# Keeping the low parts of twice-used weights, and five smaller rearrangements, in a two-block kernel on one core

## The chip, the cores and the metric

The kernel runs on one NeuronCore of one Trainium2 chip. A core has five engines with a queue of instructions each: TensorE (PE in the profile; its weight loads are listed as PEld), VectorE (DVE), ScalarE (ACT), GpSimd (POOL) and SyncE (SP). Here SP issues every large transfer between the chip's memory and the core's on-chip memory; sixteen DMA engines carry them out. The metric is the device time of one execution in microseconds, lower is better.

## The reference, cut to what matters

The input is x of 1024 tokens by 1024 features in fp32. Two blocks follow each other.

Block one: an RMS norm, one projection `w_in`, gated linear attention with 4 heads (64 key, 128 value features; decay per key feature, in the reference by chunks), a short causal convolution, the output projection `w_out`; then a gated FFN of 2816 hidden features (`w_gate_upffn`, `w_down`); then a gate `sigmoid(u3 @ w_ple_gate) * (p @ w_ple_proj)`; each added to the residual.

Block two: a layer norm, one projection `w_in_2` whose columns feed three mixers (spatial gating; a 31-tap convolution with its own layer norm over 256 channels; windowed attention with a bias by relative position), `w_out_2`, a residual and a last layer norm.

```
log_a = log_sigmoid(g_lr @ w_gate_up + b_gate) / 16
o     = causal attention of q, k, v with decay exp(cumsum(log_a))
y     = layer_norm(conv31(a * sigmoid(b)) + conv_b); yb = silu(y) * silu(gate)
```

## The kernel before, in words

Activations lie with features on the 128 partitions and 512 tokens (a half, `hf` 0 or 1) in the free dimension. fp32 products are made of three products in a faster format: each operand is split into a high part (rounded) and a low part (the rest), and `mm3` (lines 294 to 296) multiplies high by high, high by low, low by high. A product of a 1024 by 128 weight with a half is 24 matmuls of 128x512, which one reads off the profile as 24 starts in some 5.45 us; here that is called a gemm.

Weights come through the class `Weights`, in the order of a plan that is written out beforehand. `load` sends one weight (512 KB) from memory to one of three raw buffers on SP's queue; `split` makes the high part on ScalarE (line 104) and the low part on VectorE (line 105) into one of three pairs of buffers `hi` and `lo`; `ahead` splits one weight ahead of its gemm. Because a half is worked through before the other begins, `w_in`, `w_out`, `w_ple_gate` and 16 pieces of `w_in_2` stand in the plan twice and are loaded and split twice.

The order of work: `norm_in` and `proj` for half 0; then `proj` of half 1 interleaved with the attention `gla` of both halves; `out_proj` of half 0 beside what is left of `gla`; `out_proj` of half 1, beside `first_operands`; `ple_proj` beside `other_operands` (operands of the FFN: sums and differences of the two halves, each split); `ffn_up` and `ffn_down`; `ple` of half 0, then `ple` of half 1 beside `norm_mid` of half 0 (the norm that ends block one and begins block two); `mix2`, which interleaves the gemms of `w_in_2` with `norm_mid` of half 1, `spill_x2` (transposes of the residual, written to memory) and `conv31`, and ends with `conv_out`; then attention units with the last gemms (`late_tiles`) and `finish`. `run_both(a, b, na, nb)` interleaves two generators in the ratio na to nb.

What is written is an order of preference: the tile framework plans each engine's queue from it with a timing model of its own (`schedule_with_timeline_sim=True`), so an instruction may stand in its queue earlier or later than in the text. On the chip every queue runs in the order planned.

In `gla`, a chunk of 128 tokens takes two groups `g` of two heads. `exps` makes the decay factors E and multiplies: line 650 writes `qpad`, q times E for seven levels and each head of the pair apart (14 instructions of 64x64 per group; the other head's partitions hold zeros set once by line 618). `scores` first copies q into `qdiag`, a tile with zeros off the head's own partitions (line 666, GpSimd, 4 copies per chunk).

`ple_proj` begins with `load_pT`: it loads p (1 MB, line 1054), transposes it on TensorE (line 1064) and splits it. `setup2` makes a row of bias values and copies it to 128 rows for each of 8 heads, memory to memory (line 1168). `conv_out` (from line 1320) norms half 0 and then half 1: a sum over channels by a matmul with ones, the subtraction of the mean, squares (their addition on GpSimd, line 776), a second sum, `rsqrt` (lines 337 to 355), and the product with the gate.

Of the kernel before, what the change touches and what calls it, by code (L numbers as in the profile page):

```python
# [20 lines left out]
NH = 512  # L21
# [43 lines left out]
class Weights:  # L65


    RAW, SPLIT = 3, 3

    def __init__(self, nc, ctx, tc, plan):  # L70
        self.nc, self.plan = nc, plan
        self.pool = ctx.enter_context(tc.tile_pool(name="wts", bufs=1))
        self.raw, self.done = {}, {}
        self.n_raw = self.n_split = self.n_used = 0

    def load(self):
        i = self.n_raw
# [12 lines left out]
        self.raw[i] = t  # L90
        self.n_raw += 1

    def split(self):
        i = self.n_split
        if i >= len(self.plan):
            return
        while self.n_raw <= i:
            self.load()
        name, src, r0, kc, c0, m = self.plan[i]
        n = kc * m  # L100
        t = self.raw.pop(i)
        hi = self.pool.tile([128, WIDTH], F32R, tag=f"hi{i % self.SPLIT}", name=f"wh{i}")
        lo = self.pool.tile([128, WIDTH], F32R, tag=f"lo{i % self.SPLIT}", name=f"wl{i}")
        self.nc.scalar.activation(out=hi[:, :n], in_=t[:, :n], func=ACTF.Copy)  # L104
        self.nc.vector.tensor_tensor(out=lo[:, :n], in0=t[:, :n], in1=hi[:, :n].bitcast(F32), op=ALU.subtract)  # L105
        self.done[i] = (hi[:, :n].rearrange("p (k m) -> p k m", k=kc), lo[:, :n].rearrange("p (k m) -> p k m", k=kc))
        self.n_split += 1
        self.load()

    def get(self, *spec):  # L110
# [25 lines left out]
class Kernel:  # L136
    def __init__(self, tc, ctx, I, out, dbg):
        self.tc, self.nc, self.ctx, self.I, self.out, self.dbg_out = tc, tc.nc, ctx, I, out, dbg or {}
        nc = self.nc
        self.cst = ctx.enter_context(tc.tile_pool(name="cst", bufs=1))  # L140
        self.wts = Weights(nc, ctx, tc, self.weight_plan())
# [8 lines left out]
        self.dram = ctx.enter_context(tc.tile_pool(name="scr", bufs=1, space=DRAM))  # L150
# [445 lines left out]
    def gla_setup(self):  # L596
        nc, I = self.nc, self.I
        mask = self.temp([128, 448], "mask")
        nc.sync.dma_start(out=mask, in_=I["c_mask"])
        self.mask = mask.rearrange("p (l t) -> p l t", l=7).bitcast(U32)  # L600
        self.expm = self.temp([128, 1152], "expm", dtype=F32R)
        e = self.temp([128, 9, 128], "E", 2)
        nc.sync.dma_start(out=e, in_=I["c_expm"].rearrange("p (a b) -> p a b", a=9))
        nc.vector.tensor_copy(out=self.expm, in_=e.rearrange("p a b -> p (a b)"))
        self.wgu = self.temp([17, 256], "wgu")
        nc.sync.dma_start(out=self.wgu[0:16, :], in_=I["w_gate_up"][0])
        nc.sync.dma_start(out=self.wgu[16:17, :], in_=I["b_gate"])
        self.glr = self.temp([17, NH], "glr")
        nc.gpsimd.memset(self.glr, 1.0)
        self.state = self.temp([128, 2, 256], "state")  # L610
        nc.gpsimd.memset(self.state, 0.0)
        self.neg_gn = self.cst.tile([128, 1], F32, name="neg_gn")
        nc.vector.tensor_scalar(out=self.neg_gn, in0=self.v("gn_g"), scalar1=-1.0, scalar2=None, op0=ALU.mult)
        self.carry = self.temp([128, 8], "carry")
        self.qpad = [self.temp([128, 7, 2, 64], f"qpad{i}") for i in range(2)]
        self.qdiag = [self.temp([128, 2, 2, 128], f"qdiag{i}") for i in range(2)]
        for t in self.qpad + self.qdiag:
            nc.gpsimd.memset(t, 0.0)

    def gla(self, hf, R):  # L620
# [11 lines left out]
            return ap.rearrange("p g (b u n) -> p g b u n", u=2, n=n)[:, :, :, 1, :]  # L632

        def exps(c):
            for g in range(2):
# [9 lines left out]
                tok = slice(c * 128, (c + 1) * 128)  # L645
                q = qk[:, g, tok]
                for l, n in enumerate(GLA_LEVELS):
                    for par in range(2):
                        r = slice(64 * par, 64 * par + 64)
                        nc.vector.tensor_tensor(out=qs[r, l, par, :].rearrange("p (b n) -> p b n", n=n),  # L650
                                                in0=right(E[r, 1 + l, :], n), in1=right(q[r], n), op=ALU.mult)
                ql = self.temp([128, 128], "Q", 2)
                nc.vector.tensor_tensor(out=ql, in0=E[:, 8, :], in1=q, op=ALU.mult)
                k = qk[:, 2 + g, tok].rearrange("p (a t) -> p a t", a=1).to_broadcast([128, 8, 128])
                nc.vector.tensor_tensor(out=E[:, 0:8, :], in0=E[:, 0:8, :], in1=k, op=ALU.mult)
                qt = (qs, ql)
                KQ[c, g] = (E, qt)
                yield

        def scores(c):  # L660
            sT = self.temp([128, 4, 128], "sT", 2)
            tok = slice(c * 128, (c + 1) * 128)
            qd = self.qdiag[c % 2]
            for h in range(4):
                r = slice(64 * (h % 2), 64 * (h % 2) + 64)
                nc.gpsimd.tensor_copy(out=qd[r, h // 2, h % 2, :], in_=qk[r, h // 2, tok])
# [206 lines left out]
        yield from step("S4", s4)  # L873
        self.release(a11, a12)

    def ple_proj(self):

        nc, W = self.nc, self.wts
        pt = self.load_pT()
        yield  # L880
        for m in range(8):
            if m % 4 == 0:
# [47 lines left out]
    def ffn_up(self, A):  # L930
# [15 lines left out]
        for f in range(NF):  # L946
# [25 lines left out]
            nc.vector.tensor_tensor(out=u2, in0=u2, in1=s1, op=ALU.mult)  # L972
            nc.sync.dma_start(out=self.sT[f, :, 0, :], in_=u2)
            B = nxt
        for t in A.values():
            self.release(*t)
        self.release(self.up_last, *self.up_slots)
# [156 lines left out]
    def spill_x2(self, hf, N):  # L1134
# [3 lines left out]
        for t in range(4):  # L1138
            for k in range(2):
                ps = self.psx()  # L1140
                for j in range(4):
                    nc.tensor.transpose(ps[:, j * 128:(j + 1) * 128], h[k][:, j, t * 128:(t + 1) * 128], self.ident)
# [8 lines left out]
    def setup2(self):  # L1151
# [15 lines left out]
        for h in range(8):  # L1167
            nc.sync.dma_start(out=scr[h], in_=self.bias_row[h:h + 1, :].to_broadcast([128, 512]))
# [150 lines left out]
    def conv_out(self, ypad):  # L1319
# [1 line left out]
        nc = self.nc  # L1321
        a = self.cacc
        self.yb = self.bg
        for hf in range(2):
            sl = slice(hf * NH, (hf + 1) * NH)
            s = self.t512()
            nc.vector.tensor_tensor(out=s, in0=a[:, 0, sl], in1=a[:, 1, sl], op=ALU.add)
            ps = self.psx()
            self.colsum(ps, s, True)
            for ct in range(2):  # L1330
                nc.vector.scalar_tensor_tensor(out=a[:, ct, sl], in0=ps, scalar=-1.0 / 256, in1=a[:, ct, sl],
                                               op0=ALU.mult, op1=ALU.add)
            acc = self.t512()
            for ct in range(2):
                self.square_acc(acc, a[:, ct, sl], ct == 0)
            ps = self.psx()
            self.colsum(ps, acc, True)
            r = self.t512()
            self.rsqrt(r, ps, 1.0 / 256, 1e-5)
            for ct in range(2):  # L1340
# [195 lines left out]
    def run(self):  # L1536
# [3 lines left out]
        with self.banks_by(g=4, x=4):  # L1540
# [16 lines left out]
            with self.scope(4):  # L1557
# [3 lines left out]
                steps = self.out_proj(1, R[1], N[1])  # L1561
                next(steps)
                self.spill_h(0, N[0])
                run_both(steps, self.first_operands(N[0], A), 8, 8)
                self.spill_h(1, N[1])
                run_both(self.ple_proj(), self.other_operands(N, A), 18, 15)
                self.release(self.stat)
                self.ffn_up(A)
                self.ffn_down(N)
            with self.scope(5):  # L1570
                self.statz = self.slot([128, 2, NH], F32, "statz", base=True)
                for _ in self.ple(0, N[0]):
# [78 lines left out]
```

## Time and profile before

| | |
|---|---|
| median of 3 runs | 1714.7 us (1714.58 to 1716.91) |
| the profiled execution | 1713.7 us, of which the span from first to last instruction is 1711.7 us |
| busy share of the span | PE 97%, PEld 81%, DVE 67%, ACT 45%, POOL 20% |
| mean granted TensorE clock | 0.987 of full speed |
| moved by DMA | 199.83 MB, mean 117 GB/s |

TensorE is nearly always busy, so the time is its work plus the gaps in it. Its clock has two levels, 2.4 and 1.2 GHz; a granted clock of 0.66 over a stretch means that for two thirds of the stretch it was at half speed. A gap costs its own length, and what is run at 1.2 GHz after it.

### The profile page before, as it was taken

The numbers are of one execution on the slowest core, as the hardware profiler recorded it, in microseconds if no ns is written. First come the engines' busy times: TensorE is split into PE (matmuls) and PEld (weight loads), VectorE is DVE, ScalarE is ACT, GpSimd is POOL, SyncE is SP. The second block draws the span as 40 slices with busy tenths as digits, with TensorE's granted clock in tenths as the row PEclk, the third lists the DMA queues.
The fourth block names the chain that finished last, engine by engine and source line by source line (L and its number), as shares of the span: only waits on it lengthen the run. The fifth ranks groups of instructions, "written<-read, shape, count | busy, mean of one in ns | idle before, by whom it ended". The sixth has DMA issues, their size and how long they took to land.

```text
span 1711.7 us, 21055 instructions
## 1 busy us (share of the span) xinstructions
PE 1660.5 (97%) x7865; PEld 1379.6 (81%) x7865; DVE 1139.7 (67%) x1774; ACT 768.0 (45%) x1219; POOL 347.4 (20%) x293
## 2 busy tenths in 40 slices
PE   8999999999989999999999999999979999989998
PEld 6888987788767888888888888888858898878876
DVE  4255876996897645565554444237997799566997
ACT  5533346334555333333333433224677532476663
POOL 2010100200037534443330002003000010022443
PEclk9999999999999999999999999999989999999999
DMA  9333222223633222222226961342432521434111
GB/s 283 85 99 123 76 63 62 87 87 115 220 136 100 93 91 81 80 81 92 81 92 253 371 210 64 111 136 80 142 120 80 185 62 38 123 111 185 50 64 60
DMA packets 209501, 199.83 MB, mean 117 GB/s; under 512 B 9270, under 2 KB 173512, under 8 KB 207864
## 3 DMA queue, kind: packets, MB, share of 16 engines
q1 hardware_dynamic: 209400, 198.49, 35.7%
q8 instruction: 62, 1.02, 0.2%
q14 instruction: 39, 0.32, 0.1%
HBM read 157.56 MB, written 43.01 MB: 117 GB/s over the span
## 4 chain that ended last, share of the span: by engine, by line
PE 88%; DVE 7%; ACT 2%; issue 1%; DMA 1%; POOL 0%; SPq 0%; DVEq 0%; ACTq 0%; POOLq 0%
PE g L295 20%; PE g L294 20%; PE g L296 20%; PE x L294 6%; PE x L296 6%; PE x L295 6%; PE x L678 1%; PE s L1426 1%; PE t L1457 1%; PE o L1464 1%; PE x L640 1%; DVE wl L105 1%; DVE qpad L650 1%; PE x L366 1%; PE x L700 0%
## 5 line engine op out<-in xcount | busy, mean ns | idle before, releaser
L294 PE MATMUL g<-ah,wh 128*128 128x512 f32 x896 | 354.2, 399 | 11.3 <-issue 8.8
L295 PE MATMUL g<-al,wh 128*128 128x512 f32 x896 | 353.9, 396 | 0.4 <-DVE al L318 0.4
L296 PE MATMUL g<-ah,wl 128*128 128x512 f32 x896 | 353.5, 396 | 0.0
L104 ACT ACTIVATE wh<-wr 128x1024 fp32r<-128x1024 f32 (+1 forms) x142 | 150.3, 1062 | 284.8 <-PE g L295 167.5
L105 DVE TENSOR_TENSOR wl<-wr,wh 128x1024 fp32r<-128x1024 f32 (+1 forms) x142 | 181.2, 1278 | 137.5 <-ACT wh L104 133.6
L294 PEld LDWEIGHTS g<-ah,wh 128*128 128x128 f32 x896 | 169.5, 190 | 49.8 <-issue 11.2
L295 PEld LDWEIGHTS g<-al,wh 128*128 128x128 f32 x896 | 169.6, 189 | 37.5 <-issue 1.9
L296 PEld LDWEIGHTS g<-ah,wl 128*128 128x128 f32 x896 | 169.4, 189 | 37.3 <-issue 2.2
L315 DVE TENSOR_TENSOR s<-sr,s 128x1024 fp32r<-128x1024 f32 x36 | 43.8, 1223 | 69.1 <-ACT s L314 69.1
L914 POOL TENSOR_TENSOR sr<-wr,wr 128x512 f32<-128x512 f32 x22 | 47.0, 2138 | 178.3 <-DMA wr<-w_gate_upffn 142.6
L1316 DVE SCALAR_TENSOR_TENSOR cacc<-ypad,vec,cacc 128x1024 f32<-128x1024 f32 x60 | 76.1, 1293 | 0.4
L959 POOL TENSOR_TENSOR t<-t,t 128x512 f32<-128x512 f32 x22 | 39.9, 1815 | 173.4 <-ACT t L942 173.4
L314 ACT ACTIVATE s<-sr 128x1024 fp32r<-128x1024 f32 x36 | 37.8, 1054 | 77.8 <-PE x L296 59.3
L776 POOL TENSOR_TENSOR stat<-t,stat 128x512 f32<-128x512 f32 x14 | 23.5, 1703 | 234.6 <-ACT t L775 234.6
L295 PE MATMUL g<-s,wh 128*128 128x512 f32 x176 | 68.5, 389 | 0.0
L296 PE MATMUL g<-s,wl 128*128 128x512 f32 x176 | 68.5, 389 | 0.0
L295 PE MATMUL x<-s,wh 128*128 128x512 f32 x176 | 68.5, 389 | 0.0
L296 PE MATMUL x<-s,wl 128*128 128x512 f32 x176 | 68.5, 389 | 0.0
L294 PE MATMUL g<-s,wh 128*128 128x512 f32 x176 | 67.5, 389 | 0.0
L294 PE MATMUL x<-s,wh 128*128 128x512 f32 x176 | 67.5, 389 | 0.0
L650 DVE TENSOR_TENSOR qpad<-E,qk 64x64 f32<-64x64 f32 x224 | 51.4, 229 | 9.1 <-ACT E L642 6.3
L296 PE MATMUL g<-wh,al 128*128 128x256 f32 (+1 forms) x192 | 55.0, 288 | 0.0
(366 smaller groups left out, 3916.4 us busy)
## 6 DMA issues: line engine op xcount, KB each, us to landing
wr<-w_in SPq DMA_DIRECT2D x86, 512.0 KB
wr<-w_gate_upffn SPq DMA_DIRECT2D x44, 512.0 KB
sr<-sT SPq DMA_DIRECT2D x36, 512.0 KB
sT<-t SPq DMA_DIRECT2D x44, 256.0 KB
wr<-w_down SPq DMA_DIRECT2D x22, 512.0 KB
wr<-w_out SPq DMA_DIRECT2D x16, 512.0 KB
w2s<-w SPq DMA_DIRECT2D x8, 1024.0 KB
wr<-w_ple_gate SPq DMA_DIRECT2D x16, 512.0 KB
```

The source lines that it names most:

```text
L104: self.nc.scalar.activation(out=hi[:, :n], in_=t[:, :n], func=ACTF.Copy)
L105: self.nc.vector.tensor_tensor(out=lo[:, :n], in0=t[:, :n], in1=hi[:, :n].bitcast(F32), op=ALU.subtract)
L294: mm(out=ps, lhsT=lh, rhs=rh, start=start and i == 0, stop=False)
L295: mm(out=ps, lhsT=lh, rhs=rl, start=False, stop=False)
L296: mm(out=ps, lhsT=ll, rhs=rh, start=False, stop=stop and i == n - 1)
L314: nc.scalar.activation(out=hi, in_=src, func=ACTF.Copy)
L315: (eng or nc.vector).tensor_tensor(out=lo, in0=src, in1=hi.bitcast(F32), op=ALU.subtract)
L650: nc.vector.tensor_tensor(out=qs[r, l, par, :].rearrange("p (b n) -> p b n", n=n), in0=right(E[r, 1 + l, :], n), in1=right(q[r], n), op=AL ...
L776: (eng or nc.gpsimd).tensor_tensor(out=acc, in0=sq, in1=acc, op=ALU.add)
L914: nc.gpsimd.tensor_tensor(out=t13[:, 0, :], in0=b12, in1=b11, op=ALU.subtract)
L959: nc.gpsimd.tensor_tensor(out=v5, in0=v5, in1=z7, op=ALU.add)
L1316: nc.vector.scalar_tensor_tensor(out=acc, in0=src, scalar=w, in1=acc, op0=ALU.mult, op1=ALU.add)
```

## The change

Weights: when a weight stands in the plan a second time, the low part of its first use is stored in memory after the split (`keep`) and loaded into the `lo` buffer for the second use (`load_low`, asked for one weight ahead); VectorE makes no low part then. By the plan this is so for 24 pieces of `w_in`, 8 of `w_out`, 8 of `w_ple_gate` and 16 of `w_in_2`. In `gla` the copies into `qdiag` move from `scores` to the head of `exps`, and one multiplication of 128x(2x64) per level takes both heads from `qdiag`, zeros included, in place of two of 64x64. `load_pT` is called before `out_proj` of half 1 goes on. The bias copies move into `ffn_up`, one for each of f = 2 to 9. The first of each four transposes of `spill_x2` is kept in program order. `conv_out` takes each step for both halves before the next step, and its additions of squares go to VectorE. The interleaving of `ple(1)` with `norm_mid(0)` goes from 8:18 to 7:18.

```diff
@@ class Weights
+        for i, (name, _, *spec) in enumerate(plan):
+            key = (name, *spec)
+            if key in seen:
+                t = dram.tile([128, spec[1] * spec[3]], F32, name=f"low{i}")
+                self.kept[seen[key]] = self.again[i] = t
+            seen[key] = i
+    def load_low(self, i):
+        if i in self.again and i not in self.low:
+            _, _, _, kc, _, m = self.plan[i]
+            t = self.low[i] = self.low_tile(i)
+            self.nc.sync.dma_start(out=t[:, :kc * m].bitcast(F32), in_=self.again[i])
+    def keep(self):
+        if self.to_keep is not None:
+            i, lo = self.to_keep
+            self.nc.sync.dma_start(out=self.kept[i], in_=lo.bitcast(F32))
+            self.to_keep = None
@@ def split
             self.load()
+        self.keep()
...
         self.nc.scalar.activation(out=hi[:, :n], in_=t[:, :n], func=ACTF.Copy)
-        self.nc.vector.tensor_tensor(out=lo[:, :n], in0=t[:, :n], in1=hi[:, :n].bitcast(F32), op=ALU.subtract)
+        self.load_low(i)
+        lo = self.low.pop(i, None)
+        if lo is None:
+            lo = self.low_tile(i)
+            self.nc.vector.tensor_tensor(out=lo[:, :n], in0=t[:, :n], in1=hi[:, :n].bitcast(F32), op=ALU.subtract)
+            if i in self.kept:
+                self.to_keep = i, lo[:, :n]
...
         self.n_split += 1
+        self.load_low(i + 1)
         self.load()
@@ def gla_setup
-        for t in self.qpad + self.qdiag:
+        for t in self.qdiag:
             nc.gpsimd.memset(t, 0.0)
@@ def gla: exps (the same loop of copies leaves scores)
+            qd = self.qdiag[c % 2]
+            for h in range(4):
+                r = slice(64 * (h % 2), 64 * (h % 2) + 64)
+                nc.gpsimd.tensor_copy(out=qd[r, h // 2, h % 2, :], in_=qk[r, h // 2, tok])
...
-                    for par in range(2):
-                        r = slice(64 * par, 64 * par + 64)
-                        nc.vector.tensor_tensor(out=qs[r, l, par, :].rearrange("p (b n) -> p b n", n=n),
-                                                in0=right(E[r, 1 + l, :], n), in1=right(q[r], n), op=ALU.mult)
+                    e = E[:, 1 + l:2 + l, :].to_broadcast([128, 2, 128])
+                    nc.vector.tensor_tensor(out=qs[:, l].rearrange("p g (b n) -> p g b n", n=n),
+                                            in0=right(e, n), in1=right(qd[:, g], n), op=ALU.mult)
@@ def ffn_up (and the loop over 8 heads leaves setup2)
+            if 2 <= f < 10:
+                nc.sync.dma_start(out=self.bias_scr[f - 2], in_=self.bias_row[f - 2:f - 1, :].to_broadcast([128, 512]))
@@ def spill_x2
+                    if j == 0:
+                        self.tc.keep_in_program_order(ins)
@@ def conv_out
-        for hf in range(2):
+        for sl in halves:
             s = self.t512()
...
-                self.square_acc(acc, a[:, ct, sl], ct == 0)
+                self.square_acc(acc, a[:, ct, sl], ct == 0, nc.vector)
...
+        for sl, ps in zip(halves, accs):
             r = self.t512()
             self.rsqrt(r, ps, 1.0 / 256, 1e-5)
@@ def run
                 self.spill_h(0, N[0])
+                pt = self.load_pT()
                 run_both(steps, self.first_operands(N[0], A), 8, 8)
                 self.spill_h(1, N[1])
-                run_both(self.ple_proj(), self.other_operands(N, A), 18, 15)
+                run_both(self.ple_proj(pt), self.other_operands(N, A), 18, 15)
...
-                run_both(self.ple(1, N[1]), self.norm_mid(0, N[0]), 8, 18)
+                run_both(self.ple(1, N[1]), self.norm_mid(0, N[0]), 7, 18)
```

## Rows read from the trace of the kernel before

**Rows 1.** The page: span, busy time by engine, engines on the chain of waits.

```profile
span 1711.7 us, 21055 instructions
...
PE 1660.5 (97%) x7865; PEld 1379.6 (81%) x7865; DVE 1139.7 (67%) x1774; ACT 768.0 (45%) x1219; POOL 347.4 (20%) x293
...
PE 88%; DVE 7%; ACT 2%; issue 1%; DMA 1%; POOL 0%; SPq 0%; DVEq 0%; ACTq 0%; POOLq 0%
```

**Rows 2.** Busy time by stretch: length, busy by engine (instructions), granted clock, DMA share, GB/s.

```profile
5.00:35.00 30.00, 27.61 (x119) 22.13 (x120) 15.72 (x26) 21.85 (x35) 2.04 (x2) 1.00 1.04 333
285.00:320.00 35.00, 30.80 (x125) 23.04 (x124) 33.56 (x67) 19.48 (x26) 7.83 (x8) 0.95 0.27 80
350.00:365.00 15.00, 13.36 (x72) 11.61 (x71) 14.54 (x28) 7.10 (x15) 1.29 (x1) 0.89 0.42 141
440.00:455.00 15.00, 12.86 (x43) 8.14 (x42) 10.69 (x16) 5.15 (x7) 0.00 (x0) 0.89 0.75 254
475.00:520.00 45.00, 35.53 (x137) 25.75 (x136) 41.05 (x61) 24.89 (x43) 20.41 (x5) 0.92 0.37 131
...
1265.00:1285.00 20.00, 9.34 (x26) 5.36 (x26) 18.56 (x30) 16.51 (x25) 0.00 (x0) 0.66 0.27 81
1495.00:1510.00 15.00, 10.07 (x35) 7.45 (x34) 7.71 (x14) 9.44 (x14) 4.88 (x5) 0.77 0.68 210
```

**Rows 3.** Groups by line, whole span (the third row: one line's min/median/max ns).

```profile
L105 DVE TENSOR_TENSOR wl<-wr,wh 128x1024 fp32r<-128x1024 f32 (+1 forms) x142 | 181.2, 1278 | 137.5 <-ACT wh L104 133.6
...
L650 DVE TENSOR_TENSOR qpad<-E,qk 64x64 f32<-64x64 f32 x224 | 51.4, 229 | 9.1 <-ACT E L642 6.3
...
L653 DVE TENSOR_TENSOR Q<-E,qk x16: 291/292/293, 174.2 to 401.8; 128x128 f32<-128x128 f32 x16
```

**Rows 4.** 285 to 320 us: TensorE's longest wait, low parts, one of them beside GpSimd.

```profile
PE x L640 <- DVE t L347: 2.0, 1, 2.0
...
L105 DVE TENSOR_TENSOR wl<-wr,wh 128x1024 fp32r<-128x1024 f32 x4 | 6.0, 1490 | 0.0
...
302.02 2.31 DVE L105 TENSOR_TENSOR wl<-wr,wh 128x1024 fp32r<-128x1024 f32 x1
...
301.58 1.67 POOL L569 TENSOR_TENSOR y<-y,rb 128x512 f32<-128x512 f32 x1 [10.18 <-DVE y L567]
```

**Rows 5.** 437 to 488 us: SP's transfers, low parts, the wait for the p operand.

```profile
439.61 2.90 SPq L766 DMA_DIRECT2D h<-xT  x2
...
455.54 5.04 SPq L1168 DMA_DIRECT2D bias_scr<-bias_row  x8
...
L105 DVE TENSOR_TENSOR wl<-wr,wh 128x1024 fp32r<-128x1024 f32 x7 | 8.9, 1293 | 0.2 <-ACT wh L104 0.2
...
PE g L295 <- DVE pT L315: 3.3, 1, 3.3
...
482.77 1.87 DVE L315 TENSOR_TENSOR pT<-x,pT 128x512 fp32r<-128x512 f32 x3
...
PE x L420 <- DMA t<-conv_w: 1.0, 1, 1.0
```

**Rows 6.** Around 1266 us: TensorE's longest wait; VectorE's groups from 1232 to 1274.

```profile
PE g L294 <- issue: 8.8, 1, 8.8
...
L105 DVE TENSOR_TENSOR wl<-wr,wh 128x1024 fp32r<-128x1024 f32 x7 | 8.5, 1220 | 0.2 <-ACT wh L104 0.2
...
1274.48 0.81 ACT L1128 ACTIVATE ah<-h,vec 128x512 fp32r<-128x512 f32 x1
```

**Rows 7.** The end of `conv_out`: its start, GpSimd's addition, TensorE's wait, the next stage.

```profile
1462.72 0.69 DVE L1327 TENSOR_TENSOR t<-cacc 128x512 f32<-128x512 f32 x1
...
1496.27 1.28 POOL L776 TENSOR_TENSOR t<-t,t 128x512 f32<-128x512 f32 x1 [21.92 <-ACT t L775]
...
PE s L1426 <- DVE t L338: 1.9, 1, 1.9
...
1498.80 0.84 ACT L1420 ACTIVATE qs<-q 64x256 fp32r<-64x256 f32 x2
```

More of the change, by code (lines that the diff above doesn't have):

```diff
@@ L68, with __init__ @@
     RAW, SPLIT = 3, 3
-    def __init__(self, nc, ctx, tc, plan):
+    def __init__(self, nc, ctx, tc, plan, dram):
         self.nc, self.plan = nc, plan
         self.pool = ctx.enter_context(tc.tile_pool(name="wts", bufs=1))
-        self.raw, self.done = {}, {}
+        self.raw, self.low, self.done = {}, {}, {}
         self.n_raw = self.n_split = self.n_used = 0
+        seen = {}
+        self.kept, self.again = {}, {}
+        for i, (name, _, *spec) in enumerate(plan):
[5 more added lines that the diff above has]
+        self.to_keep = None
     def load(self):
@@ L91, in load, with low_tile @@
         self.n_raw += 1
+    def low_tile(self, i):
+        return self.pool.tile([128, WIDTH], F32R, tag=f"lo{i % self.SPLIT}", name=f"wl{i}")
+    def load_low(self, i):
[7 more added lines that the diff above has]
+            self.nc.sync.dma_start(out=self.kept[i], in_=lo.bitcast(F32))
+            self.to_keep = None
     def split(self):
@@ L102, in split @@
         hi = self.pool.tile([128, WIDTH], F32R, tag=f"hi{i % self.SPLIT}", name=f"wh{i}")
-        lo = self.pool.tile([128, WIDTH], F32R, tag=f"lo{i % self.SPLIT}", name=f"wl{i}")
         self.nc.scalar.activation(out=hi[:, :n], in_=t[:, :n], func=ACTF.Copy)
-        self.nc.vector.tensor_tensor(out=lo[:, :n], in0=t[:, :n], in1=hi[:, :n].bitcast(F32), op=ALU.subtract)
+        self.load_low(i)
[5 more added lines that the diff above has]
+                self.to_keep = i, lo[:, :n]
         self.done[i] = (hi[:, :n].rearrange("p (k m) -> p k m", k=kc), lo[:, :n].rearrange("p (k m) -> p k m", k=kc))
         self.n_split += 1
+        self.load_low(i + 1)
         self.load()
@@ L140, in __init__ @@
         self.cst = ctx.enter_context(tc.tile_pool(name="cst", bufs=1))
-        self.wts = Weights(nc, ctx, tc, self.weight_plan())
+        self.dram = ctx.enter_context(tc.tile_pool(name="scr", bufs=1, space=DRAM))
+        self.wts = Weights(nc, ctx, tc, self.weight_plan(), self.dram)
         self.base = ctx.enter_context(tc.tile_pool(name="base", bufs=1))
@@ L149, in __init__ @@
         self.psum = self.banks = None
-        self.dram = ctx.enter_context(tc.tile_pool(name="scr", bufs=1, space=DRAM))
         self.n_name = 0
@@ L634, in exps @@
         def exps(c):
+            tok = slice(c * 128, (c + 1) * 128)
+            qd = self.qdiag[c % 2]
+            for h in range(4):
+                r = slice(64 * (h % 2), 64 * (h % 2) + 64)
+                nc.gpsimd.tensor_copy(out=qd[r, h // 2, h % 2, :], in_=qk[r, h // 2, tok])
             for g in range(2):
@@ L644, in exps @@
                 qs = self.qpad[(2 * c + g) % 2]
-                tok = slice(c * 128, (c + 1) * 128)
                 q = qk[:, g, tok]
                 for l, n in enumerate(GLA_LEVELS):
-                    for par in range(2):
-                        r = slice(64 * par, 64 * par + 64)
-                        nc.vector.tensor_tensor(out=qs[r, l, par, :].rearrange("p (b n) -> p b n", n=n),
-                                                in0=right(E[r, 1 + l, :], n), in1=right(q[r], n), op=ALU.mult)
+                    e = E[:, 1 + l:2 + l, :].to_broadcast([128, 2, 128])
+                    nc.vector.tensor_tensor(out=qs[:, l].rearrange("p g (b n) -> p g b n", n=n),
+                                            in0=right(e, n), in1=right(qd[:, g], n), op=ALU.mult)
                 ql = self.temp([128, 128], "Q", 2)
@@ L663, in scores @@
             qd = self.qdiag[c % 2]
-            for h in range(4):
-                r = slice(64 * (h % 2), 64 * (h % 2) + 64)
-                nc.gpsimd.tensor_copy(out=qd[r, h // 2, h % 2, :], in_=qk[r, h // 2, tok])
             ps = self.psx()
@@ L874, in other_operands, with ple_proj @@
         self.release(a11, a12)
-    def ple_proj(self):
+    def ple_proj(self, pt):
         nc, W = self.nc, self.wts
-        pt = self.load_pT()
         yield
@@ L1141, in spill_x2 @@
                 for j in range(4):
-                    nc.tensor.transpose(ps[:, j * 128:(j + 1) * 128], h[k][:, j, t * 128:(t + 1) * 128], self.ident)
+                    ins = nc.tensor.transpose(ps[:, j * 128:(j + 1) * 128], h[k][:, j, t * 128:(t + 1) * 128], self.ident)
+                    if j == 0:
+                        self.tc.keep_in_program_order(ins)
                 o = self.t512()
@@ L1166, in setup2 @@
         scr = self.dram.tile([8, 128, 512], F32, name="bias_scr")
-        for h in range(8):
-            nc.sync.dma_start(out=scr[h], in_=self.bias_row[h:h + 1, :].to_broadcast([128, 512]))
         self.bias_scr = scr
@@ L1323, in conv_out @@
         self.yb = self.bg
-        for hf in range(2):
-            sl = slice(hf * NH, (hf + 1) * NH)
+        halves = [slice(hf * NH, (hf + 1) * NH) for hf in range(2)]
+        sums = []
+        for sl in halves:
             s = self.t512()
             nc.vector.tensor_tensor(out=s, in0=a[:, 0, sl], in1=a[:, 1, sl], op=ALU.add)
-            ps = self.psx()
-            self.colsum(ps, s, True)
+            sums.append(self.psx())
+            self.colsum(sums[-1], s, True)
+        accs = []
+        for sl, ps in zip(halves, sums):
             for ct in range(2):
@@ L1334, in conv_out @@
             for ct in range(2):
-                self.square_acc(acc, a[:, ct, sl], ct == 0)
-            ps = self.psx()
-            self.colsum(ps, acc, True)
+                self.square_acc(acc, a[:, ct, sl], ct == 0, nc.vector)
+            accs.append(self.psx())
+            self.colsum(accs[-1], acc, True)
+        for sl, ps in zip(halves, accs):
             r = self.t512()
```

## The prediction

> **What bounds the kernel now.** I read the page first: TensorE is busy for 97% of the span and makes up 88% of the chain of waits; the span is 1711.7 us of the execution's 1713.7 [rows 1]. No edit touches TensorE's arithmetic, so only time in which it waits, or runs at half clock after a wait, can be won. The table by stretch shows where that is. I count a stretch's loss as its length less TensorE's busy time, plus the busy time times what its granted clock lacks of 1. From 285 to 320 us: 4.2 idle + 0.05 x 30.8 = 5.7 us (call it A). 350 to 365: 1.6 + 1.5 = 3.1 (B). 440 to 455: 2.1 + 1.4 = 3.5 (C). 475 to 520: 9.5 + 2.8 = 12.3 (D). 1265 to 1285: 10.7 + 3.2 = 13.8 (E). 1495 to 1510: 4.9 + 2.3 = 7.2 (F) [rows 2]. Together 45.6 us; this is the most that the change can win, and every one of the six lies where the diff touches. In four of them (A, B, D, E) VectorE is busy for 91 to 97% of the stretch [rows 2], and the waits name it: the norm of the attention in A, the p operand in D [rows 4, 5]. E's 8.8 us are put down to "issue", but its end, at 1275, comes right behind the first operand of `norm_mid`, at 1274.48, so it is the norm that is late [rows 6].
>
> **Low parts kept.** 24 + 8 + 8 + 16 = 56 of 142 subtractions go, at 1278 ns each 71.6 us of VectorE [rows 3]. Most of it lies beside a full TensorE and is worth nothing; it counts where VectorE is late.
>
> A: the stretch has four of them, 6.0 us [rows 4], all of `w_in`'s second use. Joined heads: 224 multiplications at 229 ns become 112; a form of 128x128 exists in line 653 at 292 ns, so 51.4 us become 32.7, 1.2 us less for each of 16 pairs of chunk and group [rows 3]. Bounds for the unseen form: 229 (no longer than half its width: 25.7 us won) and 2 x 229 (nothing won); I take 292, the same number of elements. Two pairs fall into A: 2.3 us. So VectorE is relieved of 8.3 us of its 33.6, where TensorE's longest wait is 2.0: I take 5.0 of the 5.7 (bounds 0 and 5.7). B has no second-use weights, but inherits A's shorter queue and the joined heads: 2.5 of 3.1 (0 and 3.1).
>
> Moving the `qdiag` copies leaves their number; they are ready long before E is, and cost nothing as long as GpSimd isn't held up. Here the row says that GpSimd and VectorE disturb each other: a low part took 2.31 us beside a GpSimd product of 1.67, against the mean of 1.28 [rows 3, 4]. The Trainium skill, GPSIMD Engine Reference, section Key points, states it as a shared interface, with contention for VectorE instructions with two inputs in on-chip memory, which the joined multiplications are. By that rule each chunk could lose about the 1.0 us of this row on VectorE, which takes back some 40% of the joined heads' gain and would make A and B 6.5 us together in place of 7.5; by the rows the same copies lay beside the same kind of instruction before, and I leave 7.5.
>
> C: seven low parts between 437 and 488 us, 8.9 us [rows 5]; two are of `w_ple_proj` and stay. But here the replacement is a transfer of 512 KB in a stretch whose DMA engines are busy for 0.75 [rows 2]: two reloads of 1 MB were issued at 439.6 to 442.5, and TensorE already waits 1.0 us for a small transfer behind them [rows 5]. At this stretch's 254 GB/s 512 KB are 2.1 us; three low parts are wanted at once, and the 1 MB of p now falls here too (4.1 us). I count a cost of 3 us (bounds: 3.5 won, if the transfers come ahead of the reloads; 8 lost, if p and two low parts are waited for in full).
>
> D: the p operand is split on VectorE behind everything else; TensorE waits 3.3 us for it, and its three splits take 1.87 us there [rows 5]. Loaded and transposed earlier, it moves into a stretch where VectorE waits. What is late next is the chain of the second half's norm and the operands of the FFN, all VectorE: it is relieved of 1.9 us of splits and of the last two low parts of `w_out` (2.6), and no longer waits for a TensorE held up by 3.3. The gap itself and half of this relief: 5.5 of 12.3 (bounds 0 and 12.3).
>
> E: between 1232 and 1274 us VectorE has next to no idle time and makes seven low parts, 8.5 us [rows 6]. By the plan with three buffers, four are of `w_ple_gate`'s second use and go (4.9 us), three are first uses of `w_in_2` and stay. The ratio 7:18 puts about one more step of `ple(1)` behind the norm: five VectorE instructions at 0.69, 3.4 us. So the operands come 8.3 us earlier, against 10.7 idle; some of the half clock goes with it, but ScalarE, busy for 16.5 of 20 [rows 2], then paces the operands. I take 8.0 of 13.8 (bounds 4 and 13.8).
>
> **Convolution norm.** It starts at 1462.72 and TensorE waits for its second half at the end, after the last gemm [rows 7]. In step, the second half's latency lies beside the first's; each addition of squares goes from GpSimd's 1.28 us [rows 7] to VectorE's 0.69. F's waits on it vanish, but the next stage's own operands begin only at 1498.80 [rows 7], and behind them stand a GpSimd step and the first matmul: 4.0 of 7.2 (0 and 7.2).
>
> **Stores and loads.** 112 transfers of 512 KB are new on SP's queue. From 5 to 35 us the DMA engines are at 1.04 [rows 2]; about three stores fall there, at 333 GB/s 1.6 us each. The norm of x waits for its own stores there. Cost 1.5 us (bounds 0 and 4.7). Elsewhere the share is 0.27 to 0.42 in A, B, D, E [rows 2], and a low part is asked for one weight, some 5 us, ahead; nothing. The bias copies leave 5.0 us of SP's queue at 455 [rows 5] for the FFN, where nothing waits: nothing, though a transfer queued behind them in C or D may come earlier. The transposes of `spill_x2` in program order: nothing; bounds 2 us won in E, where some were pulled ahead of a late norm, and 5 lost if TensorE stands behind one.
>
> **Sum.** -5.0 - 2.5 + 3.0 - 5.5 - 8.0 - 4.0 + 1.5 = -20.5 us on the execution's 1713.7: 1693.2. The median of the runs stands 1.0 above that execution: 1694.2, say 1694.
>
> **The rivals.**
>
> 1. VectorE is relieved, but its place as the late engine is taken by ScalarE and by the order planned for TensorE. For it: ScalarE at 16.5 of 20 in E [rows 2]; the plan is made with a model's times. Against: in A ScalarE has 15.5 of 35 us free. Price: half of D, E and F is left, 8.75 us: 1703.
>
> 2. The other side: the low parts come late. SP's queue is in order; a low part waits for its buffer, and raw loads stand behind it. For it: the wait for a small transfer in C [rows 5]. Against: the DMA shares in A, B and E. 40 low parts (24 + 8 + 8) feed stages where TensorE has little slack; from 20.5 / 40 = 0.5 us lost at each the change is slower, half clock included; at 1.0 us each the time is 1694 + 40 = 1734, at 0.7 it is 1722.
>
> 3. No change: gaps only move, since the new plan of all queues closes some and opens others of the same size, as in C. Price: 1712 to 1718. Against: six gaps of one cause would have to return.
>
> 4. The change doesn't do what it says: the second use isn't recognised, and all 142 subtractions stay. Then A keeps the joined heads (2), E the ratio (3.4), D the p operand (3.3), F its 4: 1714.7 - 12.7 = 1702. Against: the key is name and place of the piece, and these repeat.
>
> **How the numbers follow.** Forecast 0.62, rivals 0.18, 0.08, 0.08, 0.04. A difference of 0.2%, 3.4 us, is about what can be told from no change. Faster by more: 0.62 + 0.18 + 0.04 = 0.84; within: 0.08; slower: 0.08. The range: its lower end is the sum with A, B, D, E and F at two fifths more than taken and C free (25 x 1.4 = 35, less 1.5 of start), 1681, and 3 for the half clock that goes with a closed gap, 1678. The upper end takes in rivals 1 and 4 with C at its worst bound (1703 + 5): 1708.
>
> **What would show it.** Right: line 105 (wherever it stands) 86 times, no longer 142; the granted clock at 1.00 in A and above 0.85 in E; TensorE's wait near 1266 under 3 us; no wait of 3 us for the p operand; VectorE's total down by some 90 us (71.6 + 18.7). Wrong: TensorE waiting on a transfer into `wl` many times (rival 2), a new wait near 445 longer than 8 us, or E's gap as long as now with ScalarE named.

## The result and the profile after

The changed kernel takes 1690.5 us (median of 4 runs, 1687.5 to 1691.2), the kernel before, run beside it, 1715.1 us (1714.6 to 1716.9): a ratio of 0.9851, 95% interval 0.9834 to 0.9868. A second time it took 1688.8 us, ratio 0.9852 (0.9839 to 0.9864). The profiled execution took 1690.2 us.

The page after; the last two rows are the low parts of `Weights.split` and the joined multiplication, from the view by line (busy us, mean ns):

```profile
span 1688.5 us, 21056 instructions
...
PE 1651.3 (98%) x7865; PEld 1377.1 (82%) x7865; DVE 1055.3 (62%) x1608; ACT 768.7 (46%) x1219; POOL 338.7 (20%) x289
...
L135 DVE TENSOR_TENSOR wl<-wr,wh 128x1024 fp32r<-128x1024 f32 (+1 forms) x86 | 108.1, 1258 | 115.5 <-ACT wh L130 109.7 <-DMA low<-wl 5.3
...
L686 DVE TENSOR_TENSOR qpad<-E,qdiag 128x128 f32<-128x128 f32 x112 | 26.6, 294 | 12.7 <-ACT E L680 12.5
```

Against [rows 1, 3]: VectorE lost 84 us of work: the row of low parts is 73 us shorter (142 became 86) and that of the heads 25 (224 multiplications became 112), and some 14 us of these 98 came back, in other rows and in overlap that two rows both count. TensorE has 9 us less busy time for the same 7865 instructions, at a granted clock of 0.993 over the span, 0.987 before. Now the table by stretch. The first five stretches are those of before [rows 2]; the last two lie where their work is now:

```profile
5.00:35.00 30.00, 27.64 (x117) 22.07 (x118) 16.40 (x26) 21.85 (x35) 2.05 (x2) 1.00 1.06 370
285.00:320.00 35.00, 35.00 (x181) 29.88 (x180) 26.26 (x56) 13.43 (x20) 9.41 (x9) 1.00 0.53 163
350.00:365.00 15.00, 12.80 (x63) 10.86 (x62) 14.62 (x28) 6.00 (x12) 2.21 (x1) 0.89 0.64 209
440.00:455.00 15.00, 15.00 (x73) 12.46 (x72) 14.93 (x25) 9.00 (x15) 0.00 (x0) 1.00 0.75 244
475.00:520.00 45.00, 35.42 (x135) 26.65 (x134) 40.17 (x55) 27.07 (x45) 12.04 (x6) 0.92 0.40 135
1250.00:1270.00 20.00, 15.37 (x59) 12.22 (x58) 19.82 (x32) 17.21 (x25) 0.00 (x0) 0.83 0.61 188
1475.00:1490.00 15.00, 13.54 (x62) 10.98 (x61) 5.09 (x11) 7.79 (x13) 2.89 (x4) 1.00 0.81 255
```

A and C are full, at a clock of 1.00, although the DMA share in A has doubled. In the stretches of B and D the losses, counted as in the prediction, are as large as before (3.6 and 12.4 us). E is cut from 13.8 to 7.2 (4.6 idle + 0.17 x 15.4), F from 7.2 to 1.5. TensorE's largest waits of the whole span (us in total, times, longest):

```profile
PE g L487 <- DMA x<-x: 6.4, 2, 5.3
PE g L328 <- DVE al L1164: 5.1, 2, 4.6
PE g L327 <- ACT t L923: 5.1, 3, 3.9
PE g L328 <- DVE S L348: 3.4, 1, 3.4
PE g L327 <- ACT wh L130: 2.0, 2, 1.6
```

None is for a low part that comes by DMA. The first is the kernel's start, the second what is left of E, the third and fourth are D.

To give each gain its place I use one more measure: the *lead*, the difference of the times at which two traces have done the same amount of TensorE's matmuls (each counted at the usual interval of its shape). What the lead grows by between two times of the before-trace was won there. From 560 to 1200 us, the FFN, it doesn't change in any kernel. "To 20" is the start, "to 400" holds A and B, "to 460" C, "to 560" D, "to 1400" E, "to 1580" F; behind it the lead changes by under 1.5 us, but for `no_low` and `conv_old`, which lose some 3 us there.

A minus is time won. Each median is set against executions of the kernel before that ran beside it, so kernels are best compared by their ratios.

| kernel | median us | ratio to before (95%) | to 20 | to 400 | to 460 | to 560 | to 1400 | to 1580 |
|---|---|---|---|---|---|---|---|---|
| forecast | 1694 | | +1.5 | -7.5 | +3.0 | -5.5 | -8.0 | -4.0 |
| changed | 1690.5 | 0.9851 (.9834-.9868) | +0.5 | -6.5 | -4.9 | -1.7 | -5.9 | -5.7 |
| after_again | 1688.8 | 0.9852 (.9839-.9864) | +0.4 | -6.5 | -4.9 | -3.1 | -5.6 | -5.7 |
| no_low | 1702.7 | 0.9926 (.9913-.9938) | +0.2 | -4.0 | -4.1 | -1.6 | +2.4 | -6.0 |
| heads_old | 1699.4 | 0.9910 (.9896-.9923) | 0.0 | +3.3 | -4.8 | -3.3 | -5.4 | -5.8 |
| only_low | 1708.2 | 0.9966 (.9954-.9978) | +0.5 | +5.4 | -5.1 | -1.8 | -5.8 | +0.1 |
| only_heads | 1705.2 | 0.9945 (.9932-.9957) | +1.3 | -5.7 | -4.1 | -3.3 | +0.3 | +0.2 |
| conv_old | 1697.0 | 0.9894 (.9880-.9907) | +0.3 | -6.5 | -4.9 | -2.2 | -5.7 | -0.4 |
| pt_old | 1686.3 | 0.9834 (.9818-.9850) | +0.9 | -8.0 | -5.0 | -5.4 | -5.0 | -5.7 |
| bias_late | 1688.1 | 0.9842 (.9828-.9855) | +0.1 | -6.4 | -4.9 | -3.9 | -5.5 | -5.8 |
| pt_bias | 1686.6 | 0.9838 (.9825-.9851) | +0.5 | -6.5 | -5.0 | -5.7 | -4.9 | -5.7 |
| ratio_8 | 1690.8 | 0.9864 (.9851-.9878) | +0.2 | -6.4 | -4.9 | -0.2 | -3.2 | -5.7 |
| spill_free | 1687.4 | 0.9840 (.9827-.9852) | +1.6 | -6.5 | -4.9 | -3.1 | -6.1 | -5.7 |
| pt_old_5 | 1680.8 | 0.9800 (.9788-.9813) | +0.6 | -6.5 | -5.0 | -5.6 | -11.7 | -4.6 |

The changed kernel's own row shows how far one profile can be trusted: up to 560 us it, `after_again`, `conv_old`, `ratio_8` and `spill_free` have the same code, and D comes out between -0.2 and -3.1.

### The profile page after: what moved, and what is told of

It reads as the page before. It is cut to its first block, busy times and chain, and to the rows that moved or that the text cites. A ratio compares the mean times of both kernels' runs of the same rounds, so it can differ in the third digit from the quotient of the medians.

```text
span 1688.5 us, 21056 instructions
## 1 busy us (share of the span) xinstructions
PE 1651.3 (98%) x7865; PEld 1377.1 (82%) x7865; DVE 1055.3 (62%) x1608; ACT 768.7 (46%) x1219; POOL 338.7 (20%) x289
## 5 line engine op out<-in xcount | busy, mean ns | idle before, releaser
L135 DVE TENSOR_TENSOR wl<-wr,wh 128x1024 fp32r<-128x1024 f32 (+1 forms) x86 | 108.1, 1258 | 115.5 <-ACT wh L130 109.7
L946 POOL TENSOR_TENSOR sr<-wr,wr 128x512 f32<-128x512 f32 x22 | 29.8, 1353 | 159.0 <-DMA wr<-w_gate_upffn 133.0
L328 PE MATMUL g<-S,wh 128*128 128x512 f32 x132 | 52.2, 396 | 3.4 <-DVE S L348 3.4
L327 PE MATMUL g<-wh,ah 128*128 128x256 f32 (+1 forms) x192 | 54.9, 289 | 0.0
```

Source lines behind the costliest of these rows:

```text
L327: mm(out=ps, lhsT=lh, rhs=rh, start=start and i == 0, stop=False)
L328: mm(out=ps, lhsT=lh, rhs=rl, start=False, stop=False)
L946: nc.gpsimd.tensor_tensor(out=t13[:, 0, :], in0=b12, in1=b11, op=ALU.subtract)
```

## Experiments

**Low parts and heads: four kernels.** `no_low` takes the kept low parts out of the changed kernel:

```diff
-            if key in seen:
+            if key in seen and False:
```

> The changed kernel with every low part subtracted again on VectorE (142 subtractions, no low part stored or reloaded), all other edits in place. Theory (VectorE's load of low parts is the main part of the gain): A, B, C and half of E come back, 12 to 15 us, so about 1704 us, and in the profile TensorE waits again for VectorE between 275 and 320 us and by over 7 us near 1255. Rival (the other edits carry it: joined heads, ratio, p operand, convolution norm): 3 to 4 us, about 1694, with the gap near 1255 as short as in the changed kernel (4.8 us).

`only_low` puts them alone into the kernel before (the class `Weights` of the change, nothing else):

> The kernel before with nothing changed but the low parts, which are stored at a piece's first use and reloaded at its second. Theory (the low parts are the main part and stand by themselves): what taking them out of the changed kernel cost (12 us) comes here alone: 1701 to 1705 us. Rival (they pay only together with the joined heads, the ratio and the p operand, since VectorE is still late without these): 1709 to 1713. The forecast's sum gives them A 2.7, B 1.2, C -3, D 1, E 4.9, start -1.5: 1709.

`heads_old` takes the joined heads out of the changed kernel (the diagonal copies go back to `scores` with them, and the zeros of `qpad` to `gla_setup`):

```diff
-                    e = E[:, 1 + l:2 + l, :].to_broadcast([128, 2, 128])
-                    nc.vector.tensor_tensor(out=qs[:, l]..., in0=right(e, n), in1=right(qd[:, g], n), ...)
+                    for par in range(2):
+                        r = slice(64 * par, 64 * par + 64)
+                        nc.vector.tensor_tensor(out=qs[r, l, par, :]..., in0=right(E[r, 1 + l, :], n), ...)
```

> The changed kernel with the heads' multiplications apart as before (224 of them) and the diagonal copies with the scores. Theory (A needs both, the joined heads being 2 of its 5 us): 1 to 3 us slower, about 1692.5, with TensorE waiting for VectorE again between 275 and 320. Rival (with the low parts gone VectorE has room and this part is worth nothing): within 1 us of 1690.5.

and `only_heads` puts them alone, with the diagonal copies ahead of them, into the kernel before:

> The kernel before with nothing changed but the joined heads (112 multiplications in place of 224, the diagonal copies ahead of them). Theory (they are a relief of VectorE in the two stretches A and B alone, and need no other edit: with the low parts off, the changed kernel still won 3.8 us up to 400 us): 3 to 5 us faster than before, about 1711. Rival (heads and low parts pay only together, as taking the heads out of the changed kernel cost 8.9): 1714 to 1716.

Taking the low parts out costs 12 to 14 us, as expected, but not where it was expected: 8.3 us in E, 2.5 in A and B, 0.8 in C and some 2 behind 1580 us. Alone they bring 7 (1715.4 to 1708.2), between the two theories. The forecast's own sum for them, 1709, is near that by luck: it took 3.9 us won in A and B and 3 lost in C, and the trace has 5.4 lost and 5.1 won. Taking the heads out costs 9 to 11, several times what was expected; alone they bring 10 (1715.3 to 1705.2), twice the expectation. The table gives the places. All that the joined heads bring, 11.7 us by 560, lies in A to D; in E and F they bring nothing. The low parts bring 6 to 8 us in E (`only_low` -5.8; `no_low` +2.4 where the changed kernel has -5.9) and, without the joined heads, they *lose* 5 us before 400. That loss sits in one place. Stretch 340 to 380 us, columns as in the tables by stretch, of `only_low`, then of `only_heads`, then of the changed kernel:

```profile
340.00:380.00 40.00, 32.38 (x164) 27.40 (x163) 27.45 (x64) 10.99 (x21) 3.62 (x2) 0.87 0.31 105
```

```profile
340.00:380.00 40.00, 37.82 (x210) 32.52 (x210) 28.05 (x54) 13.56 (x24) 2.16 (x2) 1.00 0.27 86
```

```profile
340.00:380.00 40.00, 37.80 (x195) 32.76 (x194) 27.54 (x61) 15.25 (x28) 2.21 (x1) 0.96 0.34 110
```

VectorE is busy for 27 to 28 us in all three, so it is not the load. The timeline of `only_low` shows the order (start, us, engine, line; in brackets the idle time before and its releaser):

```profile
361.96 1.22 DVE L688 TENSOR_TENSOR E<-E,qk 128x1024 f32<-128x1024 f32 x1
363.09 1.22 DVE L135 TENSOR_TENSOR wl<-wr,wh 128x1024 fp32r<-128x1024 f32 x1
363.32 1.13 PE L711 MATMUL x<-qpad,E 128*128 128x128 f32 x8 [2.86 <-DVE E L688]
364.23 3.25 DVE L683 TENSOR_TENSOR qpad<-E,qk 64x64 f32<-64x64 f32 x14
...
367.50 0.29 DVE L686 TENSOR_TENSOR Q<-E,qk 128x128 f32<-128x128 f32 x1
367.71 2.49 DVE L348 TENSOR_TENSOR al<-y,ah 128x512 fp32r<-128x512 f32 x4
368.45 0.79 PE L328 MATMUL g<-al,wh 128*128 128x512 f32 x1 [4.00 <-DVE al L348]
```

With less work in front of it TensorE is 5 us ahead here, and then stands 2.9 us for the scaled keys and 4.0 us for the first operand of `out_proj`. For the 4.0 us the rows show why: fourteen multiplications of the heads, 3.25 us in one row, stand ahead of the operand's low half. The idle time costs clock as well, 0.87 over the stretch. `heads_old` shows the same two waits (2.9 and 3.1 us), and the same order. But this order is new. In the kernel before, the heads' last two groups of fourteen stand behind that operand (the first of them is shown), and TensorE doesn't wait for it:

```profile
360.55 2.50 DVE L315 TENSOR_TENSOR al<-y,ah 128x512 fp32r<-128x512 f32 x4
...
364.43 3.26 DVE L650 TENSOR_TENSOR qpad<-E,qk 64x64 f32<-64x64 f32 x14
```

and in `only_heads` the last two groups of seven joined ones do:

```profile
359.51 2.49 DVE L315 TENSOR_TENSOR al<-y,ah 128x512 fp32r<-128x512 f32 x4
361.92 1.50 DVE L653 TENSOR_TENSOR qpad<-E,qdiag 128x128 f32<-128x128 f32 x7
```

In the changed kernel the last seven ahead of the operand run at 352.19 us, and TensorE's longest wait in this stretch is 1.6 us, for another operand. So the two parts are not a sum of relief: each edit gives VectorE's queue a new plan, and the plan made for the low parts alone puts the heads' work ahead of an operand that is wanted at once. By these rows an estimate: the order of before would take some 3.3 of the 4.0 us away, joined multiplications in the new order 1.8 (3.25 against 1.50). Of the 9.2 us that the lead of `heads_old` is behind that of the changed kernel at 400 us, 2.8 are there at 320, ahead of this place. How much of the heads' gain is shorter multiplications, how much the order planned and how much the diagonal copies going first was not separated.

**The convolution's norm.** `conv_old` is the changed kernel with the loop of before:

```diff
-        halves = [slice(hf * NH, (hf + 1) * NH) for hf in range(2)]
...
+        for hf in range(2):
+            sl = slice(hf * NH, (hf + 1) * NH)
...
-                self.square_acc(acc, a[:, ct, sl], ct == 0, nc.vector)
...
+                self.square_acc(acc, a[:, ct, sl], ct == 0)
...
```

> The changed kernel with the convolution's norm as before: one half after the other, the additions of squares on GpSimd. Theory (F's gain of 6 us is the norm in step): some 6 us slower than the changed kernel, about 1696.5, with the waits of TensorE between 1462 and 1490 back. Rival (F closed because the work before it was done earlier): within 1 us of 1690.5.

6.5 to 8 us slower, as expected, and the lead of F falls from -5.7 to -0.4. TensorE's waits from 1440 to 1500 us, `conv_old`:

```profile
PE s L1460 <- DVE t L371: 4.7, 1, 4.7
```

and the changed kernel:

```profile
PE g L327 <- ACT cg L1309: 1.5, 1, 1.5
```

The 4.7 us is put down to the helper of the norm's inverse root, as were the 1.9 in [rows 7]. F is the convolution norm's edit and nothing else: `only_heads` and `only_low`, which have the old norm too, win nothing there (+0.2 and +0.1). Its two halves, the norm in step and the squares added on VectorE, were taken out together and not apart.

**The p operand and the bias broadcasts.** In D the changed kernel has the wait of 3.9 us for ScalarE's `t`, the copy of a product of `ple_proj`. ScalarE's own wait there and SP's transfers in the changed kernel:

```profile
ACT t L923 <- DMA ppT<-t: 5.0, 1, 5.0
```

```profile
445.74 2.49 SPq L1008 DMA_DIRECT2D bias_scr<-bias_row  x4
...
448.90 1.97 SPq L1008 DMA_DIRECT2D bias_scr<-bias_row  x3
...
455.13 4.06 SPq L841 DMA_DIRECT2D hT<-h  x1
459.28 5.73 SPq L95 DMA_DIRECT2D wr<-w_gate_upffn  x2
468.62 0.34 SPq L841 DMA_DIRECT2D hT<-h  x1
469.95 0.34 SPq L924 DMA_DIRECT2D ppT<-t  x1
475.21 0.38 SPq L95 DMA_DIRECT2D wr<-w_gate_upffn  x1
475.71 17.77 SPq L924 DMA_DIRECT2D ppT<-t  x9
```

A buffer of the copies comes free when its store of 256 KB has landed, and the first store is issued behind 2 MB of bias copies, two stores of 1 MB and weights. The bias copies stand in the text of `ffn_up` now, but are issued at 446 us: the scheduler moves up a transfer for which nothing holds it back. `bias_late` holds them:

```diff
-                nc.sync.dma_start(out=self.bias_scr[f - 2], ...)
+                self.tc.keep_in_program_order(
+                    nc.sync.dma_start(out=self.bias_scr[f - 2], ...))
```

> The changed kernel with the eight bias broadcasts held in program order, so that they are truly issued in the FFN and no longer at 446 to 453 us, ahead of the stores of the transposed p. Theory (the wait at 477 us is for such a store that is jammed in the DMA queue by them): the wait of 5.0 us of ScalarE for ppT shrinks to under 2 us, TensorE's gap at 477 goes, 3 to 5 us faster: about 1686. Rival (other transfers in the same stretch, the reloads of 1 MB, make the jam, or the norm of the second half is late anyway): within 1 us of 1690.5.

`pt_old` loads p at the start of `ple_proj` as before:

```diff
-                pt = self.load_pT()
-                run_both(self.ple_proj(pt), self.other_operands(N, A), 18, 15)
+                run_both(self.ple_proj(), self.other_operands(N, A), 18, 15)
```

> The changed kernel with p loaded at the start of ple_proj as before, not ahead of out_proj. Theory (the early p operand is worth little, since D won only 1.3 us in all): within 2 us of the changed kernel, 1690 to 1692.5, with TensorE waiting some 3 us for the p operand and less for what follows it. Rival (the p operand was D's main gap, as forecast): 3 to 5 us slower, about 1694.5.

and `pt_bias` has both edits:

> The changed kernel with p loaded in ple_proj as before and the bias broadcasts truly in the FFN. Alone these came out at 1686.3 and 1688.1 against 1690.5. Theory 1 (both take away one and the same wait, ScalarE's 5.0 us for a store of the transposed p in a jammed DMA queue): they don't add, 1685.5 to 1688. Theory 2 (the early p costs by its own, through the place of its splits and the order of VectorE): they add, 1683 to 1684.5.

TensorE's waits from 465 to 500 us in `bias_late`:

```profile
PE g L328 <- DVE S L348: 4.8, 1, 4.8
PE g L327 <- ACT t L923: 1.4, 2, 0.7
```

and in `pt_old`:

```profile
PE g L328 <- DVE S L348: 1.9, 3, 1.2
PE g L327 <- ACT t L924: 1.4, 2, 0.7
PE g L328 <- DVE pT L348: 1.4, 1, 1.4
PE g L327 <- ACT pT L347: 0.7, 1, 0.7
```

with SP's stores there:

```profile
472.98 20.02 SPq L925 DMA_DIRECT2D ppT<-t  x12
```

The wait for the store goes in `bias_late`, as the first theory says: TensorE's 3.9 us became 0.7, where the five profiles of the changed kernel's own code have 1.8 to 4.6. But an operand of the FFN, VectorE's, is then late by 4.8 us (2.3 to 3.7 in these five). The time lies between the two theories: 1 to 2 us are won against the changed kernel, which the intervals don't separate from nothing. `pt_old` did what no theory expected: it is not slower but faster, D wins 5.4 us where the five profiles of the changed kernel's own code have -0.2 to -3.1, and by the ratios 2.5 to 3 us (0.9834 and, with `pt_bias`, 0.9838, against 0.9851 and 0.9852; the intervals of single pairs still touch). With p late TensorE waits 1.4 and 0.7 us for it, the first product of `ple_proj` is copied 2 us later, the first store goes out at 473 and not at 470, and ScalarE's wait for a store is gone. In `pt_bias` the two together win no more than the late p alone (1686.6 and 1686.3), as the theory says by which both take away the same wait; and with the bias copies held the early p (`bias_late`, 0.9842) shows no gain over the late one (`pt_bias`, 0.9838). Why the late p wins more than `bias_late` in D is not shown by this: the wait for VectorE's operand `S` is shorter with it (1.9 us in three, against one of 4.8). The waits of `pt_old`, 5.4 us in sum, are in sum hardly less than the 5.7 of `after_again`, but none is over 1.4 us, and the granted clock from 460 to 490 us is 1.00, against 0.94 there.

**The ratio of `ple(1)` to `norm_mid`.** `ratio_8` has 8:18 as before, `pt_old_5` is `pt_old` with 5:18:

```diff
-                run_both(self.ple(1, N[1]), self.norm_mid(0, N[0]), 7, 18)
+                run_both(self.ple(1, N[1]), self.norm_mid(0, N[0]), 8, 18)
```

> The changed kernel with 8 steps of ple(1) to 18 of norm_mid, as before, in place of 7. Theory (the ratio moves the operands of norm_mid by one step, 3.4 us, of which a part shows): 2 to 3.5 us slower, about 1693, with TensorE's gap near 1254 longer than 4.8 us by as much. Rival (the tile scheduler sets its own order by priority and readiness): within 1 us of 1690.5.

> The best so far (the changed kernel with p loaded in ple_proj as before, 1686.3) with 5 steps of ple(1) to 18 of norm_mid in place of 7. Theory (the gap near 1250 is the norm that comes late, and each step of ple(1) behind it is worth 1 to 1.5 us): 1683 to 1685, gap under 3 us. Rival (the gap moves, because ple(1) is then late or the scheduler places the steps by readiness): 1685.5 to 1688.

TensorE's longest wait from 1225 to 1300 us is 4.6 us in the changed kernel, and in `ratio_8`

```profile
PE g L328 <- DVE al L1164: 5.5, 1, 5.5
PE g L327 <- issue: 1.4, 1, 1.4
```

in `pt_old_5`

```profile
PE g L328 <- DVE al L1165: 1.2, 1, 1.2
```

and in `no_low`, where the ratio is 7 but VectorE makes six low parts between 1230 and 1262 us and not three,

```profile
PE g L327 <- issue: 9.9, 1, 9.9
```

In the traces one step (8 to 7) is worth some 2.5 us, but the profiled execution of `ratio_8` was its slowest (1694.3 us). By the ratios it is 2, with intervals that overlap, and the median, 1690.8, lies where the rival theory put it. Two rows of the table speak against a worth of its own: `only_low`, still at 8, wins as much in E as the changed kernel at 7 (-5.8 and -5.9), and without the low parts the kernel at 7 (`no_low`, +2.4) is no better there than the one at 8 (`only_heads`, +0.3). So the step's worth is not shown. Two more steps are worth 6 (1686.3 to 1680.8, ratios 0.9834 and 0.9800 with intervals apart), more than either theory gave. The gap did not move. `pt_old_5` is the fastest kernel of this study.

**Order of the spill transposes, and the reference of the pair.** `spill_free` lets the scheduler move the first transpose of each group again; `after_again` is the changed kernel.

```diff
-                    if j == 0:
-                        self.tc.keep_in_program_order(ins)
```

> The changed kernel with the first transposes of spill_x2 free to be moved again, as before. Theory (they are put where TensorE has work either way, costed at nothing): within 1 us of the changed kernel. Rival (held in order they kept TensorE from standing behind a late norm in E): 2 us slower.

> The changed kernel once more, on the same chip as the three others, so that differences of 2 to 4 us can be read against it. All theories: 1689.5 to 1691.5.

1687.4 against 1688.8 us, intervals 0.9827 to 0.9852 and 0.9839 to 0.9864: no difference that these runs show. `after_again` came out 0.7 us under its expectation.

## Why the prediction held, and where it did not

The forecast was 1694 us, with 1678 to 1708; the result is 1690.5. The mechanism was right in the main: VectorE was late in the stretches named, its relief filled A and C and halved E, F went with the norm's edit, and the time of the FFN stayed as it was. D was not closed. Of what was to show it, line 135 runs 86 times, A's clock is 1.00, VectorE is 84 us lighter (90 forecast, from two terms that measured 98 together), and TensorE waits for no low part. Two signs failed: the clock where E's work now lies is 0.83 and not above 0.85, and TensorE's wait there is 4.6 us and not under 3. In D the sign came, no wait of 3 us for p, but a wait of 3.9 us for a store took its place. And the sum came near partly because errors cancelled: by the table C, F and the start came out 10.6 us better than taken, D, E, A and B 6.9 worse.

- **C, the step that failed most.** I counted +3.0 for transfers in a jammed stretch; it won 4.9. C's loss was lateness handed on from the stretches ahead of it. Any relief of VectorE there clears C: it wins 4.1 with the heads alone and 5.1 with the low parts alone. The DMA share was 0.75 as before, and TensorE waited for none of it; the 1.0 us for a small transfer [rows 5] is gone too. Also p's load did not move into C: it was issued at 421.5 us before, and is at 404.6 with the early and at 405.9 with the late p; the scheduler had moved it up all along, and only its transposes and splits moved.
- **D.** I took 5.5 for the gap of the p operand and the relief behind it; 0.2 to 3.1 came in the five profiles of this code. The gap for p did go, and the jam that I had priced in C showed here instead, as a wait for the landing of a store (3.9 us, and 2.0 in `after_again`), with 3.4 us for VectorE's operand `S` behind it. The 5.4 of the kernels with the late p is my number by chance: they keep 2 us of waiting for p.
- **A and B together** were right in sum (-7.5, measured -6.5), wrong in share. The heads, to which I gave 2.3 us in A, carry it: without them there is a loss, most of it between 340 and 380 us. I had added up VectorE's busy time; what counted was which instruction the plan puts ahead of an operand that TensorE wants next. That is the mechanism of rival 3, new gaps from a new plan, at one place. The heads' own term was too small as well: VectorE has 24.8 us less of them, and I took 18.7 as number times mean duration. The joined ones take 294 ns in the mean (I took 292), but next to each other one starts 203 ns after the other (median), before that one ends: 112 x 294 ns are 32.9 us, and the row's busy time is 26.6. The 64x64 ones before, one start 232 ns after the other, did not overlap (51.4 us by either count).
- The shortest of the joined multiplications takes 276 ns, as one line's min/median/max shows:

```profile
L686 DVE TENSOR_TENSOR qpad<-E,qdiag x112: 276/284/784, 167.9 to 383.8; 128x128 f32<-128x128 f32 x112
```

  So 112 x 18 ns, 2.0 us, are lost to disturbance over the whole span at most, whatever the cause. The Trainium skill's rule on GpSimd and VectorE (GPSIMD Engine Reference, section Key points) had a price of about 1.0 us per chunk in the forecast, some 8 us over all chunks; that was too high here. That A and B came to the 6.5 us which the forecast gave by that price is chance.
- **E** won 5.9 of the 8.0 taken. The low parts are the main term, as forecast: alone they win 5.8. The step of the ratio, 3.4 in the forecast, was worth between nothing and 2.7 us. What I did not see is that the ratio could be taken further.
- **F** won 5.7, 4.0 taken: the next stage's own operands, which I had put behind the norm, were not late once the norm was done; TensorE waits 1.5 us there.
- **The start** cost 0.5 us (1.5 taken). `only_heads`, without a single store of a low part, has +1.3 there: no cost of the stores can be seen. **The spill transposes**, costed at nothing, are nothing. **The bias broadcasts**, costed at nothing, were not moved at all, and where they stay they have a part in D's wait.

Rival 2, low parts that come late, did not happen at any place of the changed kernel. It did once in `only_low`, whose two last low parts of `out_proj` are issued at 463 us, behind 2 MB of bias copies; this is the wait that ends at 471.6 us:

```profile
PE g L329 <- DMA wl<-low: 3.1, 1, 3.1
```

Rival 1 did not happen either: in D it is a store, not ScalarE's work, that took part of VectorE's place.

## What to carry to other kernels

Relief of an engine that is late does not add up. Each edit gives its queue a new plan, so ask at each gap which instructions stand there ahead of the operand that is waited for, and whether they stood there before (low parts alone lost 5 us by 400 us, where the heads then won 10). A mean duration times a number is not an engine's time where instructions overlap; the busy time is. A transfer moved in the text is moved on the chip only if something holds it; read the queue's own timeline before giving it a price. And starting a stage earlier also starts its stores earlier: here they stood behind some 4 MB in the queue, and the wait for one (1.8 to 4.6 us in five profiles) was of the size of the gap that was closed (3.3).

## What the runs showed that I had not expected

In the changed kernel prefetched loads stood a DMA share of 0.74 (400 to 430 us) and 0.83 (430 to 460) without one wait of TensorE for them, while a store on whose landing a buffer depends made ScalarE wait 5.0 us at a share of 0.57 (460 to 490). And idle time of TensorE costs more than its length: in the stretch of `only_low` from 340 to 380 us, 7.6 us of idle time come with 0.13 x 32.4 = 4.2 us of clock.
